# Expert weights as two fp16 parts made on chip, row stores issued by GpSimd, and score products on all 128 rows, in a two-layer attention and mixture-of-experts kernel

## The chip, the cores and the metric

One core of a Trainium2 chip runs the whole kernel. The metric is the device time of one execution in microseconds (us). Work runs on TensorE (PE in the profile; its weight loads are PEld), VectorE (DVE), ScalarE (ACT), GpSimd (POOL) and SyncE (SP), which here does little but issue DMAs. Sixteen DMA engines move data between memory and the chip.

## The reference, cut to what matters

Two layers. Each mixes the tokens (1024 latent ones of width 1024, and 256 context ones) by three groups of heads, of which two are attention with a softmax over scores, and then sends every token to two of 32 experts. One expert is a SwiGLU unit with three fp32 matrices of 2 MB each:

```python
s_loc = jnp.einsum('bnqhgd,bnkhd->bnhgqk', qb, kb) * ATTN_SCALE      # head width 64
...
p = softmax(concat([s_loc, s_ctx, sink_col], -1), -1)
...
def expert_block(args):
    xk, e = args            # rows of one expert; w_gate, w_up: 1024 x 512, w_down: 512 x 1024
    return (jax.nn.silu(xk @ w_gate[e]) * (xk @ w_up[e])) @ w_down[e]
```

Layer 0 sends 1280 tokens to experts, layer 1 only the 1024 latent ones.

## The kernel before

**Stages.** Each layer runs through the input projection, the recurrent heads, attention, the output projection, the routing, the experts and the combination of the experts' rows. On the span of the profiled execution, attention lies at about 732 to 1036 us in layer 0 and 2551 to 2827 us in layer 1, and the experts that are loaded by a run-time index start at 1232 and 2998 us.

**Attention.** Queries and keys are kept as a high and a low fp16 part of 64 rows each (one row for each entry of a head). The tile qs holds the high part in rows 0 to 63 and the low part in rows 64 to 127; k1 holds the keys' high part twice, in both halves; kl holds the keys' low part once, in rows 0 to 63. A score tile is the sum of a product on 128 rows (L1149: both parts of qs against k1) and one on 64 rows (L1150: the high part of qs against kl), for pieces of 256 or 128 keys. After it come the bias and maximum on DVE (L1162), the exponential on ACT (L1168), the normalization on GpSimd (L1179), transposes on PE (L1182, L1187), their copies on ACT and DVE (L1183), and the products with the values (L1192). The keys come by the DMAs k<-Bk and kl.

**Experts.** `PROFILE` and `FIXBLK` fix how many units of 32 rows each rank of expert gets. Of the 29 experts that are loaded by index, layer 0 gives 29 at least one unit, 19 at least two, 12 at least three, 12 four, 7 five, 5 six, 4 seven and 1 eight; in layer 1 the counts are 29, 18, 13, 6, 3, 2, 1, 1, 1, 1. Three more experts are fixed: their weights are loaded ahead of the stage, and they have 2, 2 and 3 units in layer 0, and 1, 2 and 1 in layer 1. In all that is 96 units in layer 0 and 79 in layer 1. An expert's units are worked in blocks of 128 rows and a rest of 64, 64 and 32, or 32 rows.

For an expert, `expert_load` issues three DMAs on SP (L1580: wg, wu, wd, 2 MB each) into one of three sets of buffers (two slots of pool wpa, and wp with wp2), taken in turn. For a block, `expert_rows` gathers the rows (L1592, an indirect DMA on GpSimd), transposes them and copies them to hT. `expert_block` multiplies them by wg and wu in fp32 (L1618). Each fp32 product appears as two instructions of the same columns. Blocks of 64 rows put wg and wu side by side in two column groups, and blocks of 32 rows use four. Its second half, `down`, applies silu (L1623), multiplies (L1624), transposes (L1628), copies gT (L1631, L1633), multiplies by wd (L1639), copies the result to y (L1643 and near) and stores it on SP (L1651 for 128 rows, L1653 for fewer). `down` of one block is issued after the first half of the next. In layer 1 the tile y has two buffers, in layer 0 three.

**What sets the order.** Instructions run in the order of each engine's queue. A DMA queue on SP also runs in order, so an SP DMA that waits for its tile holds back those behind it. `order_end` estimates the end of a sequence of experts from constants for a load and for the columns, and `expert_order` picks a sequence by it.

**After the experts**, the rows of ys are gathered on GpSimd (L1737) and combined.

## Time and profile before

| | |
|---|---|
| Median of 3 runs | 3684.35 us (3678.03 to 3684.88) |
| Profiled execution: its own time | 3684.05 us |
| Profiled execution: its span | 3682.0 us |
| PE busy | 3146.3 us (85% of the span) |
| DVE, ACT, POOL busy | 1787.3, 1090.0, 915.9 us (49%, 30%, 25%) |
| Granted TensorE clock, mean | 0.91 |
| DMA, mean over the span | 208 GB/s |

The profile gives busy time by engine, and the span in windows with the busy time, the granted TensorE clock and the busy share of the DMA engines. The averages run over stages with different limits, so the windows of a stage are read rather than the whole. In the views, L followed by a number is a line of the kernel, and "<-" behind a time of idleness names what ended it.

### The profile page before, as it was taken

Reading aid. Unit: us, or ns where it says so; the run is one execution under the profiler, and the core shown is the slowest. Engines: PE = TensorE matmul, PEld = TensorE weight load, DVE = VectorE, ACT = ScalarE, POOL = GpSimd, SP = SyncE. Lnnn points to the kernel's source line nnn. Section 1 sums busy time; section 2 is a strip of 40 time slices with the busy share of each in tenths; the row PEclk is TensorE's granted clock in tenths of the full one; section 3 lists DMA queues with packets and bytes.
Section 4 is the critical chain, followed back from the end, with each engine's and each line's share of the span. In section 5 each row is a group of like instructions: output and inputs, shape, how many; then the busy total and the mean of one; then the engine's idle time right before and its main releaser. Section 6 shows DMA issues by size and latency. Waiting matters only on the chain. (4 is left out here: it accounts for less than half of the span.)

```text
span 3682.0 us, 67190 instructions
## 1 busy us (share of the span) xinstructions
PE 3146.3 (85%) x26916; PEld 1837.6 (50%) x26916; DVE 1787.3 (49%) x4387; ACT 1090.0 (30%) x2416; POOL 915.9 (25%) x912
## 2 busy tenths in 40 slices
PE   7998889999997889999738988898999879986773
PEld 4656557656654344444326655675655444432331
DVE  4357777377668311111186677773755841110115
ACT  4333334346533100000045433442554310000001
POOL 2023433143324100000073244331432410000003
PEclk9989889989998899999968987997999879997987
DMA  9864333552264889989762533335331778899885
GB/s 361 298 185 113 88 87 95 147 152 67 79 206 166 275 334 360 368 347 358 293 223 74 158 94 98 94 89 163 96 106 57 254 238 344 330 386 360 308 317 196
DMA packets 456087, 770.06 MB, mean 209 GB/s; under 512 B 194398, under 2 KB 328830, under 8 KB 439134
## 3 DMA queue, kind: packets, MB, share of 16 engines
q1 hardware_dynamic: 442206, 718.16, 56.2%
q0 software_dynamic: 12848, 44.97, 3.8%
q8 instruction: 214, 3.51, 0.4%
q10 hardware_dynamic: 720, 2.62, 0.2%
q14 instruction: 99, 0.81, 0.1%
HBM read 650.68 MB, written 114.97 MB: 208 GB/s over the span
## 5 line engine op out<-in xcount | busy, mean ns | idle before, releaser
L1618 PE MATMUL pgate<-wg,hT 128*32 128x256 f32 (+2 forms) x1968 | 532.4, 487 | 85.9 <-issue 31.8
L1618 PEld LDWEIGHTS pgate<-wg,hT 128*32 128x32 f32 (+2 forms) x1968 | 196.3, 135 | 349.9 <-issue 287.7
L1618 PE MATMUL pgate<-wu,hT 128*32 128x256 f32 (+1 forms) x1648 | 361.6, 462 | 10.2 <-DMA wu<-w_up 10.2
L1639 PE MATMUL pd<-wd,gT 128*32 128x256 f32 (+2 forms) x1968 | 321.8, 472 | 51.7 <-DVE gT L1631 25.8
L514 PE MATMUL acc<-hL,wH 128*128 128x256 f16 (+2 forms) x1040 | 345.5, 333 | 16.3 <-POOL hL L471 16.2
L513 PE MATMUL acc<-hH,wH 128*128 128x256 f16 (+2 forms) x1040 | 343.3, 334 | 7.2 <-DVE hH L470 6.4
L515 PE MATMUL acc<-hH,wL 128*128 128x256 f16 (+2 forms) x1040 | 344.9, 333 | 0.0
L1623 ACT ACTIVATE sg<-pgate 64x256 f32<-64x256 f32 (+2 forms) x86 | 43.1, 501 | 980.3 <-PE pgate L1618 980.3
L1592 POOL DMA_INDIRECT xg<-hmoe,map x69 | 62.3, 903 | 1037.5 <-PE ptg L1628 566.3
L1179 POOL TENSOR_SCALAR s<-s,rd 128x640 f32<-128x640 f32 (+2 forms) x216 | 171.6, 795 | 288.4 <-DVE rd L1175 115.8
L1639 PEld LDWEIGHTS pd<-wd,gT 128*32 128x32 f32 (+2 forms) x1968 | 127.1, 130 | 208.7 <-issue 123.0
L1624 DVE TENSOR_TENSOR sg<-sg,pgate 64x256 f32<-64x256 f32 (+1 forms) x66 | 35.6, 540 | 344.4 <-ACT sg L1623 340.9
L1168 ACT ACTIVATE s<-s,nm 128x640 f32<-128x640 f32 (+2 forms) x216 | 164.4, 764 | 45.8 <-DVE nm L1165 39.8
L1277 PE MATMUL acco<-wo,o 128*128 128x512 f16 x756 | 176.5, 387 | 0.0
L1192 PE MATMUL po<-pt,vt 128*64 128x128 f32 x1920 | 168.6, 291 | 7.3 <-DVE pt L1183 6.5
L1618 PE MATMUL pup<-wu,hT 128*128 128x512 f32 x320 | 165.4, 605 | 9.6 <-DMA wu<-w_up 9.6
L1149 PE MATMUL pss<-k,qs 128*128 128x256 f16 (+1 forms) x552 | 153.2, 278 | 17.3 <-DMA k<-Bk 13.4
L1624 DVE TENSOR_TENSOR sg<-sg,pup 128x512 f32<-128x512 f32 x20 | 13.8, 688 | 292.1 <-PE pup L1618 292.1
L1618 PEld LDWEIGHTS pgate<-wu,hT 128*32 128x32 f32 (+1 forms) x1648 | 134.3, 123 | 42.1 <-issue 21.1
L1150 PE MATMUL pss<-kl,qs 64*128 64x256 f16 (+1 forms) x552 | 152.6, 277 | 0.0
L515 PEld LDWEIGHTS <-wL 128*128 128x128 f16 (+1 forms) x1040 | 104.9, 101 | 87.4 <-issue 26.7
L513 PEld LDWEIGHTS <-wH 128*128 128x128 f16 (+1 forms) x1040 | 105.4, 101 | 75.4 <-issue 19.7
(406 smaller groups left out, 6435.3 us busy)
## 6 DMA issues: line engine op xcount, KB each, us to landing
wu<-w_up SPq DMA_DIRECT2D x64, 2048.0 KB
wd<-w_down SPq DMA_DIRECT2D x64, 2048.0 KB
wg<-w_gate SPq DMA_DIRECT2D x64, 2048.0 KB
wmod<-w_mod SPq DMA_DIRECT2D x96, 512.0 KB
w<-w_in SPq DMA_DIRECT2D x41, 512.0 KB
ld<-ys SPq DMA_DIRECT2D x40, 384.0 KB
z<-inv SPq DMA_DIRECT2D x80, 128.0 KB
ys<-y SPq DMA_DIRECT2D x20, 512.0 KB
```

The costliest lines, as they stand in the source:

```text
L513: self.nc.tensor.matmul(ov, H[:, k, :], hh, start=k == 0, stop=False)
L514: self.nc.tensor.matmul(ov, H[:, k, :], hl, start=False, stop=False)
L515: self.nc.tensor.matmul(ov, Lo[:, k, :], hh, start=False, stop=k == KD - 1)
L1149: te.matmul(pss[:, o:o + n], qs[:, e, Q], k1[:, e, k0:k0 + n], start=True, stop=False)
L1150: te.matmul(pss[:, o:o + n], qs[0:64, e, Q], kl[:, e, k0:k0 + n], start=False, stop=True)
L1168: a.activation(s2[:, e, :nk], s2[:, e, :nk], AF.Exp, bias=nm[:, e:e + 1], scale=1.0 / SS, accum_out=den[:, e:e + 1])
L1179: g.tensor_scalar(s2[:, e, :nk], s2[:, e, :nk], rd[:, e:e + 1], SC_Q, OP.mult, OP.mult)
L1192: te.matmul(po[64 * e:64 * e + 64, 0:P], vt[:, kb, 64 * e:64 * e + 64], pt[:, e, x * P:x * P + P], start=x == 0, stop=x == len(kbs) - 1)
L1277: te.matmul(acc, o[:, zo, k] if k < KD - 1 else self.og_last[:, zo, tok], wo[:, zw, k, c], start=k == 0 and y == 0, stop=k == KD - 1 and y ...
L1592: nc.gpsimd.indirect_dma_start(out=xg[:m], out_offset=None, in_=self.h2[l], in_offset=bass.IndirectOffsetOnAxis(ap=idx, axis=0))
L1618: te.matmul(o[off + i * m:off + i * m + m, :n], hT[:, k], w[:, k, i * n:i * n + n], start=k == 0, stop=k == KD - 1)
L1639: te.matmul(o, gT[:, k, :m], wd[:, k, i * n:i * n + n], start=k == 0, stop=k == 3)
```

## The change

The change has four parts.

- **Experts.** A loaded expert with two or more units (19 in layer 0, 18 in layer 1) loads its fp32 weights into the buffers wp and wp2, which serve as a stage. `expert_split` then writes them as two fp16 parts into a slot of wpa: ACT makes the high parts (L1611, two instructions of 128 x 2048 for each matrix) and DVE the low parts (L1612, likewise). The rows hT and the silu product gT are made as two fp16 parts as well, and each fp32 product becomes three fp16 products (high by high, high by low, low by high). Experts with one unit load straight into a slot of wpa and stay in fp32, as do the fixed ones.
- **Order.** The first half of a block is cut into `gates(0)` and `gates(1)`; the silu, transposes and copy of the block before (`middle`) stand between the two. `order_end` has new constants and the rule of two slots and a stage, so the sequence of experts differs.
- **Stores.** The rows y are stored by GpSimd's queue (L1713, L1715) rather than SP's. In layer 0 ACT makes all of y, in layer 1 DVE.
- **Attention.** kl is loaded into both halves, by two DMAs, and the second score product runs on all 128 rows of qs, so it also adds low by low.

```diff
@@ order_end
-W_LOAD, W_ROWS, W_COL = 17.5, 0.75, (0.0, 6.9, 11.9, 18.8, 22.2)
+W_LOAD, W_PART = 16.5, 13.5
+W_COL = ((0.0, 6.9, 11.9, 18.8, 22.2), (0.0, 5.6, 9.6, 15.2, 17.5))
...
@@ attention
-                kl = qp.tile([64, 2, T], F16, tag="kl", name="kl", bufs=1 if B else 2)
-                nc.sync.dma_start(kl, kd[1])
+                kl = qp.tile([P, 2, T], F16, tag="kl", name="kl", bufs=1 if B else 2)
+                for z in range(2):
+                    nc.sync.dma_start(kl[64 * z:64 * z + 64], kd[1])
...
-                        te.matmul(pss[:, o:o + n], qs[0:64, e, Q], kl[:, e, k0:k0 + n], start=False, stop=True)
+                        te.matmul(pss[:, o:o + n], qs[:, e, Q], kl[:, e, k0:k0 + n], start=False, stop=True)
...
@@ experts
+    def expert_split(self, ws, wp):
...
+        for w, tag in zip(ws, ("wg", "wu", "wd")):
+            k, n = w.shape[1:]
+            t = wp.tile([P, 2, k, n], F16, tag=tag, name=tag + "p")
+            for k0 in range(0, k, k // 2):
+                c = slice(k0, k0 + k // 2)
+                nc.scalar.mul(t[:, 0, c], w[:, c], SC_W)
+                nc.vector.scalar_tensor_tensor(t[:, 1, c], w[:, c], SC_W, t[:, 0, c], OP.mult, OP.subtract)
+            out.append(t)
+        return out
...
+        parts = ((0, 0), (0, 1), (1, 0)) if split else ((None, None),)
...
+        def gates(half):
+            for k in range(4 * half, 4 * half + 4):
+                for y, (zh, zw) in enumerate(parts):
...
-                    loaded[r] = self.expert_load(l, e, wps[i % len(wps)])
+                    loaded[r] = self.expert_load(l, e, wps[2 if split(r) else 0])
+                    if split(r):
+                        loaded[r] = self.expert_split(loaded[r], wps[0][0])
...
-                nc.sync.dma_start(dst, y)
+                nc.gpsimd.dma_start(dst, y)
...
-                down = self.expert_block(l, loaded[r], hT[:, :, o:o + m], m, xp, ps, tag, ps_t, tag_t, self.ys[l][row:row + m])
+                gates, middle, down = self.expert_block(l, loaded[r], hT, o, m, xp, ps, tag, ps_t, tag_t, self.ys[l][row:row + m], split(r))
+                gates(0)
+                if pending:
+                    pending[0]()
+                gates(1)
...
+                    pending[1]()
+                pending = middle, down
```

On SP's queue in the experts of layer 0 the loads and the stores are mixed before (ys_83 is the rows' buffer of layer 0; the ISA rows are register work ahead of a DMA):

```order
L1580 DMA wu<-w_up 128x4096
L1651 DMA ys_83<-y 128x1024
L1580 ISA
L1580 DMA wd<-w_down 128x4x1024
L1580 ISA
L1580 DMA wg<-w_gate 128x4096
L1653 DMA ys_83<-y 4x32x256
```

The queue of SP now holds in this place only the loads; the stores have gone from it.

On GpSimd's queue, at the same place of the changed kernel, the stores stand between the gathers of the rows of later blocks:

```order
L1715 DMA ys_83<-y 4x32x256
L1620 DMA xg<-hmoe_79,map_13966 128x1024
L1715 DMA ys_83<-y 4x32x256
L1713 DMA ys_83<-y 128x1024
L1620 DMA xg<-hmoe_79,map_13966 96x1024
L1715 DMA ys_83<-y 2x64x512
```

Before, only the gathers (L1592) stood in this queue.

On ACT's queue in the experts of layer 0, before:

```order
L1623 ACTIVATE sg<-pgate 128x512
L1601 COPY hT<-ptx 128x4x96
L1623 ACTIVATE sg<-pgate 64x512
L1650 COPY y<-pd_14544 128x512
L1623 ACTIVATE sg<-pgate 64x256
```

And in the changed kernel (wgp, wup and wdp are the tiles of an expert's fp16 parts, made from the staged wg, wu and wd):

```order
L1611 ACTIVATE wup<-wu 128x2048 x2
L1670 ACTIVATE sg<-pgate 64x512
L1632 ACTIVATE hT<-ptx 128x8x64
L1711 ACTIVATE y<-pd_14987 128x256
L1688 CAST gT<-ptg 128x4x64
L1611 ACTIVATE wdp<-wd 128x2048 x2
L1670 ACTIVATE sg<-pgate 64x512
L1611 ACTIVATE wgp<-wg 128x2048 x2
L1632 ACTIVATE hT<-ptx 128x512 x2
```

The high parts of an expert to come now stand among the silu, the rows and the results of the experts that run.

## Rows read from the trace of the kernel before

**Rows 1.** windows: length; busy PE, PEld, DVE, ACT, POOL; PEclk, DMA share, GB/s
```profile
732.00:1036.00 304.00, 294.20 (x2276) 179.75 (x2273) 205.88 (x650) 166.73 (x453) 118.76 (x147) 0.95 0.33 93
1232.00:1823.00 591.00, 553.28 (x3256) 249.70 (x3256) 78.91 (x146) 47.79 (x93) 31.41 (x35) 0.99 0.91 350
2551.00:2827.00 276.00, 270.11 (x2058) 165.75 (x2060) 172.74 (x520) 144.15 (x370) 97.43 (x118) 0.91 0.38 111
2998.00:3586.00 588.00, 473.25 (x3266) 211.63 (x3256) 71.33 (x140) 35.63 (x74) 26.90 (x30) 0.92 0.88 341
```

**Rows 2.** timeline of PE in attention: start us, us, line, operands, shapes
```profile
863.39 0.28 PE L1149 MATMUL pss<-k,qs 128*128 128x256 f16 x1
863.60 0.28 PE L1150 MATMUL pss<-kl,qs 64*128 64x256 f16 x1
863.81 0.23 PE L1149 MATMUL pss<-k,qs 128*128 128x128 f16 x1
863.98 0.23 PE L1150 MATMUL pss<-kl,qs 64*128 64x128 f16 x1
```

**Rows 3.** timeline of PE, input projection: the same columns
```profile
51.86 0.27 PE L513 MATMUL acc<-hH,wH 128*128 128x256 f16 x1
51.97 0.27 PE L514 MATMUL acc<-hL,wH 128*128 128x256 f16 x1
```

**Rows 4.** L1149: count, ns min/median/max; in 2551:2827: busy us, mean ns, idle before
```profile
L1149 PE MATMUL pss<-k,qs x552: 219/282/421, 732.1 to 2815.7; 128*128 128x256 f16 x160, 128*128 128x128 f16 x24
...
L1149 PE MATMUL pss<-k,qs 128*128 128x256 f16 x192 | 56.8, 297 | 13.4 <-DMA k<-Bk 13.4
```

**Rows 5.** timeline of PE, expert products in fp32
```profile
1228.05 0.59 PE L1618 MATMUL pgate<-wg,hT 128*64 128x512 f32 x1
1228.05 0.59 PE L1618 MATMUL pgate<-wu,hT 128*64 128x512 f32 x1
1228.47 0.59 PE L1618 MATMUL pgate<-wg,hT 128*64 128x512 f32 x1
```

**Rows 6.** DMA issues: weights, stores of 64-row and 32-row blocks
```profile
wg<-w_gate SPq DMA_DIRECT2D x64, 2048.0 KB
...
ys<-y SPq DMA_DIRECT2D x29, 256.0 KB
...
ys<-y SPq DMA_DIRECT2D x37, 128.0 KB
```

**Rows 7.** windows late in the two expert stages, columns as rows 1
```profile
1790.00:1800.00 10.00, 9.02 (x52) 3.42 (x50) 1.56 (x3) 1.18 (x2) 0.00 (x0) 1.00 1.01 397
1815.00:1820.00 5.00, 4.64 (x66) 2.09 (x62) 0.69 (x1) 0.31 (x1) 0.00 (x0) 1.00 0.13 51
3600.00:3610.00 10.00, 0.00 (x0) 0.00 (x0) 1.34 (x2) 0.00 (x0) 0.00 (x0) 0.50 0.13 51
```

**Rows 8.** timeline: first weights issued, last products, first gather, each layer
```profile
1231.83 0.36 SPq L1580 DMA_DIRECT2D wg<-w_gate  x1
...
1821.30 1.93 PE L1639 MATMUL pd<-wd,gT 128*32 128x256 f32 x32 [0.39 <-DVE gT L1633]
...
1840.96 0.95 POOL L1737 DMA_INDIRECT cy<-ys,slot  x1 [6.18 <-DMA ys<-y]
...
2998.31 0.38 SPq L1580 DMA_DIRECT2D wg<-w_gate  x1
...
3593.48 1.93 PE L1639 MATMUL pd<-wd,gT 128*32 128x256 f32 x32 [2.69 <-DVE gT L1633]
...
3618.08 0.94 POOL L1737 DMA_INDIRECT cy<-ys,slot  x1 [93.52 <-ACT dg L1771]
```

**Rows 9.** waits of the second expert stage: us in total, times, longest
```profile
DVE y L1643 <- DMA ys<-y: 163.5, 26, 19.1
```

**Rows 10.** lines L1212 and L1213: count, ns min/median/max, shapes
```profile
L1212 ACT ACTIVATE wo<-wos x16: 1041/1060/1067, 903.7 to 2728.9; 128x1024 f16<-128x1024 f32 x16
...
L1213 DVE SCALAR_TENSOR_TENSOR wo<-wos,wo x16: 1196/1213/1564, 905.9 to 2731.1; 128x1024 f16<-128x1024 f32 x16
```

More of the change, by code (lines that the diff above doesn't have):

```diff
@@ L63, in units_of_rank @@
     return [sum(r < t for t in PROFILE[l]) for r in range(NE - NFIX)] + list(FIXBLK[l])
-W_LOAD, W_ROWS, W_COL = 17.5, 0.75, (0.0, 6.9, 11.9, 18.8, 22.2)
+SPLIT = 2
+W_LOAD, W_PART = 16.5, 13.5
+W_COL = ((0.0, 6.9, 11.9, 18.8, 22.2), (0.0, 5.6, 9.6, 15.2, 17.5))
 def order_end(units):
-    pe, dma, done = 10.0, 0.0, []
+    pe, dma, part = 10.0, 0.0, 0.0
+    slots, stage = [0.0, 0.0], 0.0
     for i, n in enumerate(units):
-        if i >= NFIX:
-            dma = max(dma, done[i - 3] if i >= 3 else 0.0) + W_LOAD
-            pe = max(pe, dma + 1.5)
-        dma += W_ROWS * n
-        pe += W_COL[4] * (n // 4) + W_COL[n % 4]
-        done.append(pe)
+        split = i >= NFIX and n >= SPLIT
+        if i < NFIX:
+            ready = 0.0
+        elif split:
+            dma = max(dma, stage) + W_LOAD
+            part = max(dma + 4.5, slots[0] + W_PART, part + W_PART)
+            ready, stage = part, part - 9.0
+        else:
+            dma = max(dma, slots[0]) + W_LOAD
+            ready = dma + 1.5
+        pe = max(pe, ready) + W_COL[split][4] * (n // 4) + W_COL[split][n % 4]
+        if i == NFIX - 1:
+            stage = pe
+        else:
+            slots = slots[1:] + [pe]
     return pe
@@ L1614, in expert_block, with part, middle @@
         h = max(q // 2, 1)
-        for k in range(KD):
-            for w, o, off in ((wg, pg, 0), (wu, pu, h * m if q > 1 else 0)):
-                for i in range(h):
-                    te.matmul(o[off + i * m:off + i * m + m, :n], hT[:, k], w[:, k, i * n:i * n + n], start=k == 0, stop=k == KD - 1)
-        def down():
-            r = h * m
-            sg = xp.tile([P, 512], F32, tag="sg", name="sg", bufs=2)
-            a.activation(sg[:r, :n], pg[:r, :n], AF.Silu)
-            v.tensor_tensor(sg[:r, :n], sg[:r, :n], (pu[r:2 * r] if q > 1 else pu)[:, :n], OP.mult)
+        r = h * m
+        parts = ((0, 0), (0, 1), (1, 0)) if split else ((None, None),)
+        def part(x, z):
+            return x if z is None else x[:, z]
+        def gates(half):
+            for k in range(4 * half, 4 * half + 4):
+                for y, (zh, zw) in enumerate(parts):
+                    for w, p, off in ((wg, pg, 0), (wu, pu, r if q > 1 else 0)):
+                        for i in range(h):
+                            te.matmul(p[off + i * m:off + i * m + m, :n], part(hT, zh)[:, k, o:o + m], part(w, zw)[:, k, i * n:i * n + n],
+                                      start=k == 0 and y == 0, stop=k == KD - 1 and y == len(parts) - 1)
+        got = {}
+        def middle():
+            sg = xp.tile([P, 512], F32, tag="sg", name="sg", bufs=2)
+            s = 1.0 / (SC_H * SC_W) if split else 1.0
+            a.activation(sg[:r, :n], pg[:r, :n], AF.Silu, scale=s)
+            pr = (pu[r:2 * r] if q > 1 else pu)[:, :n]
+            if split:
+                v.scalar_tensor_tensor(sg[:r, :n], pr, s, sg[:r, :n], OP.mult, OP.mult)
+            else:
+                v.tensor_tensor(sg[:r, :n], sg[:r, :n], pr, OP.mult)
             pt = ps_t.tile([P, 512], F32, tag=tag_t, name="ptg")
@@ L1636, in down @@
             for k in range(4):
[L1637 to L1639 removed]
+                for y, (zh, zw) in enumerate(parts):
+                    for i in range(max(q, 2)):
+                        t = (p0, p1)[i] if q == 1 else p0[i * m:i * m + m, :n]
+                        te.matmul(t, part(gT, zh)[:, k, :m], part(wd, zw)[:, k, i * n:i * n + n],
+                                  start=k == 0 and y == 0, stop=k == 3 and y == len(parts) - 1)
             y = self.yp.tile([P, D], F32, tag="y", name="y", bufs=2 if l == DEPTH - 1 else 3)
             ge = self.ge.get(q)
[L1642 to L1655 removed]
+            s = 1.0 / SC_W if split else 1.0
+            for p, c in ((p0, slice(0, n)), (p1, slice(512, 1024)))[:2 if q == 1 else 1]:
+                if ge is not None:
+                    v.scalar_tensor_tensor(y[:, c], p[:, 0:n], s, ge[:, c], OP.mult, OP.mult)
+                else:
+                    a.mul(y[:, c], p[:, 0:n], s)
+            if q == 1:
+                nc.gpsimd.dma_start(dst, y)
+            else:
+                nc.gpsimd.dma_start(dst.rearrange("t (i c) -> i t c", i=q), y[:, 0:n])
+        return gates, middle, down
     def experts(self, l, wps, xp, ps, tag, ps_t, tag_t, rest):
@@ L1712, in experts @@
                 if pending:
-                    pending()
-                pending = down
+                    pending[1]()
+                pending = middle, down
             if j == 2:
                 rest(xp, ps_t, tag_t)
-        pending()
+        for f in pending:
+            f()
         overflow()
```

58 lines of the change are left out of this document (33 added, 25 removed).

## The prediction, made before the changed kernel ran

> **What bounds the kernel now.** I read the windows of the four stages that the change touches first, then the instructions of their bound engine in order of time, then the transfers, and last how each expert stage begins and ends. The two attention stages are bound by PE: it is busy 294.20 of 304 us in layer 0 and 270.11 of 276 in layer 1, against 205.88 and 172.74 for DVE, the next engine, and a DMA share of a third [rows 1]. The two expert stages are bound by transfers. Their DMA share is 0.91 and 0.88 at 350 and 341 GB/s, while the best stretch near their end runs 397 GB/s [rows 1, 7]. PE is close behind in layer 0 (553.28 of 591 us) and not in layer 1 (473.25 of 588). DVE and ACT are nearly idle there (78.91 and 47.79 us of 591), which is the room into which the change puts its work.
>
> The missing bandwidth has a shape. Where the loads are over and only stores of short blocks run, the share is 0.13, about 2 of 16 engines, at 51 GB/s [rows 7]. There are 29 stores of 256 KB and 37 of 128 KB [rows 6], so what is behind them on those engines waits for them while the others are idle.
>
> **Attention.** The change replaces the 64-row product by a 128-row one of the same columns. Before, products of 256 columns that alternate between 128 and 64 rows start 0.21 us apart, and of 128 columns 0.17 us [rows 2]. Two 128-row fp16 products of 256 columns in the input projection start 0.11 us apart [rows 3], so 128 columns would take about 0.055 (estimate). Each of the two changes the weights as well. So both sizes lose about 0.106 us for each product if the alternation is what holds them, and there are 552 of either kind [rows 4]: 1104 x 0.106 = 117 us, or 61 and 56 us when shared by the stages' PE time. This is the upper bound. Next, what is late after it: with 233 us of PE work in layer 0, DVE's 205.88 us need 254 us at a density of 0.81, which I estimate as what this chain can keep (it holds 0.68 and 0.63 now); that gives -50. In layer 1 PE's 214 us at a density of 0.93, a little under its 0.97 now, give 230 and -46. Against this stands the second DMA of kl: PE waits 13.4 us once in layer 1 for the keys [rows 4], and one more DMA lies in the same queue. I take 6 us for it, so **-90 us**. If DVE cannot hold more than 0.70, layer 0 needs 294 us and layer 1 247, and only 10 + 29 = 39 us are gained; that is the lower bound.
>
> The order in which products follow each other is also where the Trainium skill speaks against the change: "TensorE: Matmul & The Clock Gate", Part 3 on row and column tiling, states that weight loads overlap with products in flight only when the row group differs. By it the products on all rows would not close up, and the term would be 0. The trace disagrees: the 0.11 us start to start of rows 3 is between two products on all 128 rows with different weights.
>
> **Experts, PE.** An fp32 product of 512 columns is two recorded instructions (a down product of 32 rows, 4 by 4 pieces, counts x32 [rows 8]), each 0.42 us after the one before [rows 5]: 0.86 us. Three fp16 products of 512 columns, at twice 0.11, are 0.65. A block of 128 rows has 24 products, so it falls from 20.6 to 15.6 us; a block of 64 from 10.3 to 7.8, one of 32 by 1.2. By the table of units, layer 0 splits 13, 11 and 5 such blocks (some 100 us less), layer 1 7, 14 and 8 (some 80 us less). PE then has about 455 of the 591 and 395 of the 588 us. It stands below the transfers in both layers, so I give this term nothing by itself: it is cover for the rest.
>
> **Experts, the split.** The nearest rows are the same two operations in the output projection: 1.060 us on ACT and 1.213 us on DVE for 128x1024 [rows 10]. An expert has 12 times this size: 12.7 us on ACT and 14.6 us on DVE. A load of 6.29 MB at 397 GB/s takes 15.8 us, so both splits fit under it. Over 19 and 18 experts DVE goes from 78.91 to about 356 us of work in layer 0 and from 71.33 to about 334 in layer 1. They cost nothing while they lie beside a load; the rival below says what they cost if not.
>
> **Experts, the transfers.** 29 loads of 6.29 MB and 96 units with 0.262 MB each (gather and store of 32 rows of 4 KB) are 207.6 MB in layer 0, and 203.2 MB with 79 units in layer 1. At 397 GB/s these are 523 and 512 us. Two engines carry the stores of 64-row blocks, 14 in layer 0 and 15 in layer 1, at 0.131 MB on each of the two; with these the fuller engines have about 14.6 and 14.4 MB at a sixteenth of the 397 GB/s, so 588 and 581 us. The stages have 583 us until only stores run (1232 to 1815) and 588 (2998 to 3586) [rows 1, 7]. So the two engines explain the whole loss by size. A second cause lies beside it: in layer 1 DVE waits 163.5 us for stores before it may write y [rows 9]. The change moves the stores to GpSimd's queue. What the trace of before doesn't show is which engines that queue uses for a row of 64 parts. Bounds: the same two, and no gain; or all in turn, and the whole 60 to 76 us. I take the second, since the loads then have SP's queue to themselves in any case.
>
> On the second, the Trainium skill ("DMA: Bandwidth & Descriptors", on why a DMA increments its semaphore by 16) states that a hardware queue takes the lowest-numbered engines and a software queue takes them from a cursor that goes round. The trace agrees with the first half (0.13 [rows 7]); no run here shows the other.
>
> To the 523 and 512 us come waits for the stage and the two slots: a split must have ended before the stage is refilled. Between 0 and 40 us a layer; I take 14 and 8, one short load's worth. From the last landing to PE's end I take 14 us, a split of one matrix (5 us) and a block of 64 rows. Layer 0: 1231.83 + 523 + 14 + 14 = 1783, against 1823.2 now (the last products start at 1821.30 and last 1.93) [rows 8]: -40. Layer 1: 2998.31 + 512 + 8 + 14 = 3532, against 3595.4: -63. Then the first gather of the combination, which waits for the stores, comes 17.7 us after PE's end in layer 0 and 22.7 in layer 1 (1840.96 and 3618.08 [rows 8]). These are short stores one behind the other, 5 us for 256 KB at 51 GB/s. With spread stores I take 11 us, so -7 and -12. **Layer 0 -47, layer 1 -75.** At 40 us of waits they are -21 and -43.
>
> **Stores on GpSimd** cost that engine an issue for each block, beside gathers of 0.9 us. A store that waits for its y holds back the gathers queued behind it, and through them the transposes of a later block. In the order of the changed kernel the gathers stand some three blocks ahead of their use, so 30 us and more of PE's work cover it, and I cost it at nothing; without the cover it would be the wait for one block's second half, some 5 us each.
>
> **The sum**, against the profiled execution's own 3684.05 us (its span is 3682.0; the median of the runs is 3684.35, so it is a typical one): -90 - 47 - 75 = -212, **3472 us**. A measurement of this kernel can tell about 0.2%, 7 us, from no change.
>
> **The rivals.**
>
> *DVE's chain bounds attention.* Against the main case only the attention term changes, to -39: 3523 us. For it: DVE, ACT and GpSimd follow each other in every block, and DVE is at 0.68 already. Against it: PE waits for next to nothing now. Chance 0.13.
>
> *Products on all rows don't close up* (the page's rule above). Attention gives 0: 3684 - 122 = 3562 us. The trace speaks against it [rows 3]. Chance 0.04.
>
> *The stores move their queue and not their engines*, so that this part of the change doesn't do what it says. The loads keep their 583 and 588 us; attention and the shorter ends remain: 3684 - 90 - 19 = 3575 us. Chance 0.10.
>
> *More than that.* Attention at its upper bound of 117, no waits for slots, tails of 5 us: -117 - 67 - 89 gives 3411 us. Chance 0.11.
>
> *Slower: splits stand ahead of the running expert.* ACT and DVE run their queues in order. If a split of wd, say, stands ahead of the silu of the running block and its weights haven't landed, silu, gT and PE wait: 2.1 MB of landing at 397 GB/s (5.3 us) and 4.9 us for four DVE pieces, 10.2 us. For 37 experts that is 377 us, and with the other terms 3684 + 377 - 212 = 3849 us. It decides from 212/37 = 5.7 us an expert on. For it: the two queues in the order shown have the splits among the silu and the copies. Against it: the split stands after a silu whose products come later than the landing at the pace of the loads. Chance 0.05. A half of this price that just eats the gain, 3684 us, has 0.02.
>
> **How the numbers follow.** The main case has 0.55 and its own range is 3435 to 3505 us, by 30 us of waits for slots and 7 to 27 us of attention either way. The range of 8 in 10 takes in the main case, DVE's chain, the rule and the unmoved engines (0.82): 3420 to 3580 us. It leaves out the larger gain and the two bad ones. Faster 0.93, same 0.02, slower 0.05.
>
> **What would show it.** Attention: starts of the score products 0.11 us apart, the stages at 254 and 230 us and DVE's density near 0.8; with unchanged starts the term is wrong, with close starts and idle PE it is DVE's chain. Experts: windows at about 390 GB/s, PE at 455 and 395 us, DVE at 356 and 334, no wait of DVE for ys; a share of 0.13 where only stores run would say that the engines are unmoved, and PE waiting for silu behind a split would say the slower rival. The forecast is wrong if the expert stages end later than 1810 and 3575 us less what attention gave ahead of them.

## The result, and the profile after

The changed kernel takes 3565.44 us (median of 4 runs, 3555.23 to 3581.03), against 3682.19 us of the kernel before (4 runs, 3678.03 to 3684.88): a ratio of 0.9688, 95% interval 0.9667 to 0.9710. That is 117 us less. The prediction had 3472 us and the range 3420 to 3580: the time lies in the range, near its slow end, but 60 us outside the main case's own 3435 to 3505, and the gain is little more than half of the 212 us that the sum gave. The profiled execution took 3569.75 us (span 3568.1).

The page of the changed kernel: the busy time by engine, then the span in 40 slices with the busy tenths of PE, DVE and ACT, the granted clock, and the DMA engines' share.

```profile
PE 2943.9 (83%) x28620; PEld 1838.5 (52%) x28620; DVE 2283.7 (64%) x4614; ACT 1544.1 (43%) x2769; POOL 996.8 (28%) x998
...
PE   7998888989997888888737988898889867777875
DVE  4257777467768474547688677783776845555765
ACT  4334344346633153546544434343465314434641
PEclk9989899989998889899868988899899978889977
DMA  9864343372455889999862432443732769999976
```

PE fell by 202 us of work and DVE rose by 496. In the expert stages PE is at 0.8 in most slices of the first (the 14th to the 20th) and at 0.7 in most of the second (the 33rd to the 39th).

The windows of the four stages, with the columns of [rows 1], the expert stages from the first load issued to the last product:

```profile
734.00:1004.00 270.00, 244.20 (x2270) 182.45 (x2268) 201.85 (x651) 165.05 (x453) 119.28 (x146) 0.94 0.40 112
1199.50:1779.20 579.70, 489.00 (x4068) 238.39 (x4064) 323.23 (x243) 292.99 (x293) 72.88 (x76) 0.92 0.94 358
2501.50:2742.00 240.50, 213.63 (x2065) 164.14 (x2066) 172.79 (x520) 142.19 (x371) 99.13 (x118) 0.94 0.47 133
2910.60:3499.90 589.30, 451.26 (x4284) 228.46 (x4280) 327.20 (x278) 249.94 (x227) 64.02 (x73) 0.85 0.91 344
```

Set beside [rows 1], the attention stages became shorter by 34 and 36 us (303.7 to 269.9 and 276.6 to 240.4 from the first to the last product). The expert stages took 591.4 and 597.1 us from first load to last product before, and take 579.7 and 589.4 now. Their DMA share is 0.94 and 0.91, against 0.91 and 0.88 in [rows 1].

The last products and the first gather of the combination, in layer 0 and in layer 1, which answer to [rows 8]:

```profile
1775.75 3.50 PE L1702 MATMUL pd<-wd,gT 128*32 128x256 f32 x32 [1.15 <-DMA wd<-w_down]
...
1787.95 1.03 POOL L1814 DMA_INDIRECT cy<-ys,slot  x1 [5.68 <-DMA ys<-y]
...
3496.43 3.51 PE L1702 MATMUL pd<-wd,gT 128*32 128x256 f32 x32 [2.72 <-DMA wd<-w_down]
...
3508.65 1.02 POOL L1814 DMA_INDIRECT cy<-ys,slot  x1 [6.46 <-DMA ys<-y]
```

The gather comes 8.7 us after PE's end in both layers (17.7 and 22.7 before).

Put together by matched points (first score product, last attention product, first expert product, last expert product, first gather, end of the span), the difference of the two spans is this:

| stretch | forecast, us | measured, us |
|---|---|---|
| start to the first score product | 0 | +1.9 |
| attention, layer 0 and layer 1 | -90 in all | -33.8 and -36.2 |
| attention to experts, both layers | 0 | -0.6 |
| experts, first to last product | -40 and -63 | -11.7 and -9.6 |
| last product to first gather | -7 and -12 | -9.0 and -14.0 |
| gather to attention of layer 1, gather to the end | 0 | +3.5 and -4.4 |
| all | -212 | -114 |

So 82 of the missing 98 us are missing in the two expert stages.

### The profile page after: what moved, and what is told of

The parts are those of the page before. It is cut to its first block, busy times and chain, and to the rows that moved or that the text cites. A ratio compares the mean times of both kernels' runs of the same rounds, so it can differ in the third digit from the quotient of the medians.

```text
span 3568.1 us, 71262 instructions
## 1 busy us (share of the span) xinstructions
PE 2943.9 (83%) x28620; PEld 1838.5 (52%) x28620; DVE 2283.7 (64%) x4614; ACT 1544.1 (43%) x2769; POOL 996.8 (28%) x998
## 5 line engine op out<-in xcount | busy, mean ns | idle before, releaser
L1662 PE MATMUL pgate<-wgp,hT 128*64 128x512 f16 (+2 forms) x1704 | 371.7, 388 | 130.8 <-ACT wgp L1611 76.6
L1662 PEld LDWEIGHTS <-hT 128*64 128x64 f16 (+2 forms) x3408 | 210.9, 110 | 365.9 <-issue 195.5
L1662 PE MATMUL pgate<-wup,hT 128*32 128x256 f16 (+1 forms) x1224 | 212.8, 362 | 24.5 <-DVE wup L1612 13.7
L1702 PE MATMUL pd<-wdp,gT 128*64 128x512 f16 (+2 forms) x1704 | 213.1, 358 | 21.7 <-DVE gT L1689 14.9
L1612 DVE SCALAR_TENSOR_TENSOR wgp<-wg,wgp 128x2048 f16<-128x2048 f32 x74 | 166.6, 2286 | 93.4 <-ACT wgp L1611 93.4
L1612 DVE SCALAR_TENSOR_TENSOR wdp<-wd,wdp 128x2048 f16<-128x2048 f32 x74 | 166.6, 2288 | 71.8 <-ACT wdp L1611 71.8
L1612 DVE SCALAR_TENSOR_TENSOR wup<-wu,wup 128x2048 f16<-128x2048 f32 x74 | 166.2, 2287 | 31.1 <-ACT wup L1611 31.0
L1611 ACT ACTIVATE wgp<-wg 128x2048 f16<-128x2048 f32 x74 | 137.6, 1903 | 74.1 <-DMA wg<-w_gate 56.7
L1611 ACT ACTIVATE wdp<-wd 128x2048 f16<-128x2048 f32 x74 | 137.2, 1902 | 73.7 <-DMA wd<-w_down 69.3
L1715 POOL DMA_DIRECT2D ys<-y x66 | 51.8, 784 | 384.4 <-DVE y L1709 215.5
L1611 ACT ACTIVATE wup<-wu 128x2048 f16<-128x2048 f32 x74 | 137.3, 1904 | 44.4 <-DMA wu<-w_up 41.7
```

What stands on the lines that cost most here:

```text
L1611: nc.scalar.mul(t[:, 0, c], w[:, c], SC_W)
L1612: nc.vector.scalar_tensor_tensor(t[:, 1, c], w[:, c], SC_W, t[:, 0, c], OP.mult, OP.subtract)
L1662: te.matmul(p[off + i * m:off + i * m + m, :n], part(hT, zh)[:, k, o:o + m], part(w, zw)[:, k, i * n:i * n + n], start=k == 0 and y == 0, ...
L1702: te.matmul(t, part(gT, zh)[:, k, :m], part(wd, zw)[:, k, i * n:i * n + n], start=k == 0 and y == 0, stop=k == 3 and y == len(parts) - 1)
```

## The experiments

The lengths of the stages in the table are those of one profiled execution, from the first expert product to the last. Where a stretch is said to go from the first load, it starts later than that: by some 10 us in layer 0 and 16 to 18 in layer 1 in most kernels, and by 1 us in layer 0 of e5 and e6, whose first products are fewer. Experts of layer 1 in e9 are left out, since the rows of layer 0 are other numbers there and change the routing; in e5 and e6 the same holds, and layer 1 is given for its transfers alone.

| kernel | time, us | ratio to before, 95% | experts L0, L1, us |
|---|---|---|---|
| before | 3682.19 | 1 | 601.2, 614.7 |
| changed | 3565.44 | 0.9688 (0.9667 to 0.9710) | 589.5, 605.1 |
| e1: before + attention | 3599.71 | 0.9783 (0.9754 to 0.9811) | 600.2, 625.2 |
| e2: before + GpSimd stores | 3614.12 | 0.9824 (0.9793 to 0.9855) | 581.1, 581.7 |
| e3: changed, SP stores | 3615.60 | 0.9834 (0.9790 to 0.9879) | 621.3, 631.7 |
| e4: changed, no split | 3516.81 | 0.9554 (0.9521 to 0.9587) | 565.6, 577.9 |
| e5: before, few products | 3677.09 (one run) | | 599.9, 597.0 |
| e6: e5 + GpSimd stores | 3528.59 (one run) | | 542.4, 538.7 |
| e7: changed, high parts alone | 3457.66 (one run) | | 547.3, 555.6 |
| e8: changed, one product of three | 3485.11 (one run) | | 557.8, 573.1 |
| e9: changed, no low parts, three products | 3512.06 (one run) | | 559.2 |
| e10: split of 5 units and more | 3623.56 | 0.9842 (0.9820 to 0.9864) | 637.5, 617.2 |
| e11: e4 with two sets | 3583.34 (one run) | | 601.1, 597.2 |
| e12: e4, other planner constants | 3503.45 | 0.9506 (0.9473 to 0.9540) | 566.9, 566.4 |

My first reading of the two traces was theory B: the DMA engines are at 0.94 already, so the transfers have a floor near 555 us that the prediction had missed with its 397 GB/s, and the stores' engines matter little. The first four runs were made to test that against the prediction's own step.

**e1, attention alone.**

```diff
-                kl = qp.tile([64, 2, T], F16, tag="kl", name="kl", bufs=1 if B else 2)
-                nc.sync.dma_start(kl, kd[1])
+                kl = qp.tile([P, 2, T], F16, tag="kl", name="kl", bufs=1 if B else 2)
+                for z in range(2):
+                    nc.sync.dma_start(kl[64 * z:64 * z + 64], kd[1])
...
-                        te.matmul(pss[:, o:o + n], qs[0:64, e, Q], kl[:, e, k0:k0 + n], start=False, stop=True)
+                        te.matmul(pss[:, o:o + n], qs[:, e, Q], kl[:, e, k0:k0 + n], start=False, stop=True)
```

> The kernel before with the attention part of the change alone (kl in both halves, the second score product on all 128 rows). Theory A (what the two traces show: products close up to 0.11 us, and the stages get 34 and 36 us shorter because PE then waits for DVE's chain now and then): about 70 us less than before, 3612 us. Rival (the prediction's term, the shortfall in the changed kernel being due to the other parts): 90 us less, 3592 us.

Measured: 80 us less, just between the two (70 to 91 by the interval), so the run decides for neither. The attention stages are 265.3 and 237.9 us from first to last product, 77 us less in all. The experts of layer 1 came out 10 us longer to their last product, but the first gather follows it after 12.0 us in place of 22.7: from the first expert product to that gather it is 637.3 us, and 637.4 before, so nothing was lost there.

**e2, the stores alone.**

```diff
-                nc.sync.dma_start(dst, y)
+                nc.gpsimd.dma_start(dst, y)
...
-                nc.sync.dma_start(dst.rearrange("t (i c) -> i t c", i=q), y[:, 0:n])
+                nc.gpsimd.dma_start(dst.rearrange("t (i c) -> i t c", i=q), y[:, 0:n])
```

> The kernel before with the stores of rows moved to GpSimd's queue alone. Theory B (the engines' work per byte, about 555 us of all sixteen in each expert stage, and not two overfull engines, bounds the transfers; the short ends after PE's last product are the gain): 20 to 35 us less than before, about 3655 us, expert stages from first load to last product 580 to 595 us. Rival (the prediction's step: two engines overfull with 64-row stores hold the loads): stages 540 to 560 us and 90 to 110 us less in all, about 3580 us.

Measured: 66 us less, twice and more what theory B gave. The stages got 20 and 33 us shorter. From first load to last product, as the numbers above are meant, they are 571.3 and 564.1 us: below theory B's 580 to 595 and above the rival's 540 to 560. In fp32, though, PE alone has some 550 us of products in layer 0, so in that layer this run cannot tell what the transfers could do.

**e3, the changed kernel with the stores back on SP.** The edit is that of e2 backwards.

> The changed kernel with the stores of rows back on SP's queue. Theory B: the expert stages stay within 15 us each and the ends come back (9 and 18 us): 3590 to 3600 us. Rival (two overfull engines): the stages get 20 us and more longer each: 3620 us or more.

Measured: 3615.60 us, 50 us more than the changed kernel, and the stages 32 and 27 us longer. That is the rival's number for the stages, while the time lies between the two (3600 and 3620). Theory B is in doubt from the other side too.

**e4, no split.** Everything else is as in the changed kernel, but for the planner, whose rule and constants are those of before, and the three sets, which are taken in turn as before.

```diff
-SPLIT = 2
+SPLIT = 99
...
-W_LOAD, W_PART = 16.5, 13.5
-W_COL = ((0.0, 6.9, 11.9, 18.8, 22.2), (0.0, 5.6, 9.6, 15.2, 17.5))
+W_LOAD, W_ROWS, W_COL = 17.5, 0.75, (0.0, 6.9, 11.9, 18.8, 22.2)
...
-                    loaded[r] = self.expert_load(l, e, wps[2 if split(r) else 0])
+                    loaded[r] = self.expert_load(l, e, wps[i % len(wps)])
```

> The changed kernel without the split: all experts in fp32, three sets of buffers in turn and the planner's constants as before; attention, stores and the place of the silu are as in the changed kernel. Theory B (transfers bound the expert stages, so the split buys little): within 15 us of the changed kernel, 3555 to 3580 us. Rival C (PE's 553 of 591 us held layer 0, and the split is what gave its gain): 20 us or more slower than the changed kernel, 3585 us or more. Rival D (the split's stage and two slots hold back loads): 15 us or more faster, 3550 us or less.

Measured: 3516.81 us, 49 us faster than the changed kernel, and the intervals of the two ratios lie apart. This is rival D's number: the split, which was the largest part of the change, costs time, together with the order of experts that goes with it. The windows of e4's expert stages, columns as before, from first load to last product:

```profile
1197.90:1753.70 555.80, 552.67 (x3252) 250.13 (x3248) 55.38 (x103) 69.78 (x134) 63.02 (x76) 1.00 0.97 373
2875.70:3436.80 561.10, 486.86 (x3389) 213.51 (x3387) 75.94 (x148) 36.65 (x76) 60.49 (x73) 0.94 0.95 360
```

In layer 0 PE is busy 552.67 of 555.80 us in fp32: without the split PE is the bound there, at a full clock, and still the stage is 24 us shorter than with it.

**e5 and e6, the transfers alone.** To see what the transfers do when nothing holds them, most products were left out of the kernel before: of each sum over 8 or 4 pieces only the first was multiplied. e6 has GpSimd's queue for the stores besides, as in e2.

```diff
-        for k in range(KD):
+        for k in range(1):
...
-            for k in range(4):
+            for k in range(1):
```

> The kernel before with most expert products left out: only the first of the 8 and of the 4 pieces of the inner dimension is multiplied, in every block, so that PE is out of the way and the loads, gathers and stores run at their own pace. Read is layer 0, from the first load to the last product (591 us before). Theory B: 550 to 570 us. Rival (two engines overfull with the 64-row stores): 580 to 590 us. Rival C (PE holds the stage, the transfers could do 397 GB/s): about 530 us.

> The same with the stores of rows on GpSimd's queue. Theory B: within 10 us of the run with stores on SP. Rival (two overfull engines): 50 us and more shorter than that run.

Measured, layer 0 from first load to last product, e5 and then e6:

```profile
1223.00:1821.80 598.80, 251.07 (x932) 103.38 (x932) 84.53 (x167) 48.47 (x95) 33.39 (x35) 0.58 0.90 346
```

```profile
1221.10:1762.40 541.30, 261.54 (x932) 107.34 (x932) 83.83 (x167) 47.84 (x95) 65.35 (x77) 0.59 1.00 384
```

With PE at less than half of its work e5 still takes 598.8 us, no less than the kernel before (591.4; from the first product on, 599.9 and 601.2): there the stores on SP's queue were the bound. Moving them alone takes 57.5 us off, and the DMA share goes from 0.90 to 1.00 and the rate from 346 to 384 GB/s. Theory B falls. The two overfull engines of the prediction hold up in size in layer 0 (588 us forecast for the fuller engines, 598.8 measured to the last product), and so does its floor (523 us of transfers and 14 at the end, measured 541.3 in all).

The midst of e5's stage also has stretches in which only two or three of the sixteen engines work (a share of 0.16 is 2.6 engines), such as this one, with nothing on PE:

```profile
1476.00:1481.00 5.00, 0.00 (x0) 0.00 (x0) 0.00 (x0) 0.00 (x0) 0.00 (x0) 0.50 0.16 64
```

By the times of the packets in the traces, exactly two are in flight for 7% of e5's stage and for 1% of e6's, and there is next to no time with none. The same edit also takes the stores out of the loads' queue, where a store that waits for its y holds back the loads behind it (SP waits 102 us for the tiles of stores in e5). The runs don't part this from the overfull engines.

**e7, e8 and e9, the split taken apart.** All three are the changed kernel. e7 has no low parts of weights (DVE's half of the split) and one product in place of three; e8 keeps the whole split and has one product; e9 has no low parts, but three products, each with the high part.

```diff
-                nc.vector.scalar_tensor_tensor(t[:, 1, c], w[:, c], SC_W, t[:, 0, c], OP.mult, OP.subtract)
...
-        parts = ((0, 0), (0, 1), (1, 0)) if split else ((None, None),)
+        parts = ((0, 0),) if split else ((None, None),)
```

> The changed kernel with only the high parts of the split weights: DVE makes no low part of a weight, and one product stands in place of three for the split experts (the two products with low parts are left out). The rest of the chain, load to stage, ACT's split, slot, is kept. Read are the expert stages from the first load to the last product (580 us in layer 0). Theory B: 555 to 575 us, since the transfers alone take that. Rival D (the split's chain and the slots that PE frees hold the loads back): 540 us or less.

> The changed kernel with the split whole (ACT's high and DVE's low parts are made), but one product in place of three for the split experts (the products with low parts are left out). Read are the two expert stages from the first expert product to the last (589.5 and 605.1 us in the changed kernel, 547.3 and 555.6 with the high parts alone). Theory D1 (the split on DVE is the long step between a slot that comes free and the next product): 575 us or more in layer 0. Rival D2 (the time of PE's products, which holds the slots, and not the split on DVE): 555 us or less.

> The changed kernel with no low parts of the weights, but three products all the same (each with the high part): PE's time is kept, DVE's part of the split is gone. Theory D1: 555 us or less in layer 0. Rival D2: 575 us or more. If both matter in turn, between 555 and 575 in this run and in the run with one product.

Measured, layer 0 from first load to last product, e7, e8, e9:

```profile
1190.00:1727.60 537.60, 326.59 (x2440) 148.76 (x2440) 70.77 (x130) 292.51 (x294) 63.79 (x77) 0.75 0.99 385
```

```profile
1190.00:1738.20 548.20, 331.38 (x2436) 150.93 (x2432) 322.93 (x243) 292.28 (x293) 71.24 (x76) 0.75 0.99 378
```

```profile
1193.50:1742.90 549.40, 478.62 (x4068) 240.77 (x4064) 70.91 (x129) 292.82 (x293) 62.84 (x76) 0.93 0.98 378
```

With neither, layer 0 takes 537.6 us at a DMA share of 0.99, which is rival D's number: the stage and the slots, with ACT's half of the split and the changed kernel's order of experts, are no hindrance there by themselves. Taking away DVE's half alone gives 549.4 us, PE's two products alone 548.2, and the changed kernel with both has 579.7. So neither D1 nor D2 is right alone. In layer 0 either of them is nearly hidden; together they are not (10.6 us and 11.8 us from e7, but 42.1 for both). By the numbers given ahead for layer 0 (555 and less, 575 and more, from the first product) both runs fall between, 557.8 and 559.2, as the text for e9 allowed. In layer 1 DVE's half costs more by itself: 573.1 us in e8 against 555.6 in e7. Each of the three is a single run.

**e11, two sets of buffers.** e4 with two sets for the loaded experts in place of three:

```diff
-                    loaded[r] = self.expert_load(l, e, wps[i % len(wps)])
+                    loaded[r] = self.expert_load(l, e, wps[0])
```

> The kernel without a split (3517 us) with two sets of buffers for the loaded experts in place of three. Read are the two expert stages from the first expert product to the last (565.6 and 577.9 us with three sets, 589.5 and 605.1 in the changed kernel, whose products see two slots). Theory E (the split costs its time because products are left with two sets and the loads run less far ahead): both stages at or above the changed kernel's, 590 us or more and 605 us or more. Rival (the third set matters little; the splits' work is the cost): within 10 us of 565.6 and 577.9.

Measured: 601.1 and 597.2 us, against 565.6 and 577.9 with three sets: 55 us for the two stages, and 66 us more in all, by one run. The sequence of experts is still the one that the planner made for three sets. Layer 0 is above the changed kernel, as theory E has it, and layer 1 is 8 us below it. The third set is worth 20 to 35 us a layer in this kernel. In layer 0, from the first load:

```profile
1203.20:1793.00 589.80, 564.06 (x3228) 250.41 (x3228) 55.18 (x103) 69.78 (x134) 63.03 (x76) 0.98 0.92 351
```

**e10, a split for the largest experts only.** Experts of five units and more are split (10 in all), the others stay in fp32 and take whichever of the three sets was used longest ago; the planner's constants are those of before.

```diff
-SPLIT = 2
+SPLIT = 5
...
-                    loaded[r] = self.expert_load(l, e, wps[2 if split(r) else 0])
+                    if split(r):
+                        k, sets[:] = 2, [sets[1], i, -9]
+                    elif sets[0] < sets[2]:
+                        k, sets[:] = 0, [sets[1], i, sets[2]]
+                    else:
+                        k, sets[2] = 2, i
+                    loaded[r] = self.expert_load(l, e, wps[k])
```

> The changed kernel with a split only for experts of five or more units (7 in layer 0, 3 in layer 1); the others go in fp32 through all three sets of buffers, the set that was used longest ago first, with the planner's constants as before. Theory D (what the split costs goes with the number of split experts, 37 here down to 10, while PE's relief in layer 0 stays for the largest): about the time without a split, 3517 us, or up to 15 us below it, 3500 to 3520 us. Rival (each split of a large expert holds its slot and the stage as before): 3535 us or more.

Measured: 3623.56 us, 107 us more than with no split at all, the rival's number. The theory that the cost goes with the number of split experts falls. A split expert takes two of the three sets, the stage while it loads and a slot as long as it runs, and here an fp32 expert may sit in the stage, so that a load to be split waits for that expert's last product. In layer 0 from the first expert product PE has 539.88 us of work in 638 us and the DMA engines a share of 0.86:

```profile
1175.00:1813.00 638.00, 539.88 (x3824) 250.19 (x3824) 164.94 (x190) 161.59 (x209) 64.49 (x78) 0.92 0.86 326
```

That the sets are the cause here is argued from the code; the planner, which knows nothing of the split in this kernel, may have its part, and the run does not separate the two.

**e12, e4 with the planner's constants as measured.**

```diff
-W_LOAD, W_ROWS, W_COL = 17.5, 0.75, (0.0, 6.9, 11.9, 18.8, 22.2)
+W_LOAD, W_ROWS, W_COL = 16.0, 0.67, (0.0, 6.9, 11.9, 18.8, 22.2)
```

> The kernel without a split (3517 us) with the planner's two transfer constants as the runs with GpSimd stores measured them (16.0 us a load and 0.67 us a unit in place of 17.5 and 0.75), which moves the expert of ten units in layer 1 from the head of the sequence towards its middle. If the order in layer 1 (PE without a pause for its first 180 us, then transfers without a pause) costs what lies between 577.9 us and the 539 us of the run with products left out: 15 to 25 us less, 3495 to 3502 us. If not: within 8 us of 3517 us.

Measured: 3503.45 us, 13 us less than e4 by the medians, with intervals of the two ratios that overlap (0.9473 to 0.9540, and 0.9521 to 0.9587). It lies between the two numbers given ahead, so the run doesn't settle what the order costs. The stage of layer 1 went from 577.9 to 566.4 us. What was looked for in e4's layer 1 were windows like these two, of 60 us each, early and late:

```profile
2978.00:3038.00 60.00, 60.00 (x308) 27.32 (x301) 8.92 (x16) 4.07 (x8) 6.50 (x8) 1.00 0.91 360
3218.00:3278.00 60.00, 44.85 (x422) 18.91 (x418) 7.59 (x17) 2.79 (x6) 7.06 (x9) 0.91 1.02 380
```

Early, PE is never free and the DMA engines are at 0.91; late, the DMA engines are full and PE waits a quarter of the time. The new sequence moves the largest expert away from the head. Of the kernels that leave no product out this is the fastest, and it has no split: by its ratio some 182 us below the kernel before.

## Why the prediction came out as it did

**The range held, in part by luck.** The main case's own range, 3435 to 3505 us, was missed by 60 us. The wide range reached up to 3580 for the sake of two rivals, products on all rows that don't close up (3562) and stores that don't change their engines (3575). Neither came about: the time lies where they would have put it for other reasons, the split above all. Of its own signs, layer 0's experts should have ended by 1776 us (1810 less 34) and ended at 1779.25; layer 1's ended at 3499.9, before 3505. The sum of the faster rival is also 6 us off: its terms give -70 and -92 in place of -67 and -89, so 3405 us.

**Attention: the mechanism held, the size was 10 to 20 us off.** The score products start 0.11 to 0.12 us apart, as [rows 3] had it, and not 0.21 (TensorE in attention of the changed kernel; start, length, line, operands, shapes):

```profile
834.02 0.28 PE L1163 MATMUL pss<-k,qs 128*128 128x256 f16 x1
834.14 0.27 PE L1164 MATMUL pss<-kl,qs 128*128 128x256 f16 x1
834.25 0.38 PE L1201 MATMUL pp<-c,s 128*128 128x128 f32 x2
834.47 0.27 PE L1163 MATMUL pss<-k,qs 128*128 128x256 f16 x1
834.58 0.27 PE L1164 MATMUL pss<-kl,qs 128*128 128x256 f16 x1
```

PE's work fell by 50.0 us in layer 0 (294.20 to 244.20; 61 forecast) and by about 57 in layer 1 (56 forecast). In layer 0 the term that was mis-sized is mainly this work: 244.20 us are left where the sum took 233. In layer 1 it is the density that was left, 0.89 where the sum took 0.93 (in layer 0 0.905 for 0.917), with DVE at 0.75 and 0.72 of the two stages, where the sum took 0.81 for layer 0. By itself this part takes 77 us off the two stages (e1; 80 us in all), in the changed kernel 70. The rival of DVE's chain (-39) did not come about. Nor did the Trainium skill's rule ("TensorE: Matmul & The Clock Gate", Part 3, weight loads overlap only between differing row groups): by it the starts would have stayed apart. But the prediction argued against it from the wrong pair: the two products of [rows 3] have the same weights, wH, and so have the two score products at 834.47 and 834.58 (qs). The rows that follow in the kernel before show it, since there the weights change from wH to wL and back:

```profile
51.97 0.27 PE L514 MATMUL acc<-hL,wH 128*128 128x256 f16 x1
52.08 0.27 PE L515 MATMUL acc<-hH,wL 128*128 128x256 f16 x1
52.19 0.27 PE L513 MATMUL acc<-hH,wH 128*128 128x256 f16 x1
```

These are products on all 128 rows with different weights, and they too start 0.11 us apart.

**The stores: right.** The step said that two engines carry the short blocks' stores and hold the loads, that the floor without this is 523 us, and that GpSimd's queue might not have it. e5 and e6 agree with each of the three: 598.8 us at 346 GB/s with the stores on SP, two packets at a time in its poor stretches, and 541.3 us at 384 GB/s without. The Trainium skill's sentence on software queues ("DMA: Bandwidth & Descriptors", on why a DMA increments its semaphore by 16: engines from a cursor that goes round) agrees with this, though no row here names the engines, and the 0.13 of [rows 7] says only that they are about two. In e2 the move gives 66 us by itself. In the changed kernel undoing it costs 50 (e3).

**PE's work in the experts as cover: right in direction, not in size.** PE has 489.00 us of work in layer 0, where 455 was forecast, and 451.26 in layer 1, where 395 was. The forecast took its products from rows at a full clock; the granted clock of the stages is 0.92 and 0.85. In the trace 64.1 of the 489.0 us and 127.0 of the 451 lie at a clock of 0.50 (1.2 GHz), and fp16 products of 512 columns on 128 rows start 0.426 us apart there, against 0.216 at 1.00 (2.4 GHz). With that part halved the work would be 457 and 388 us (estimates), close to the forecast. Before, the clock was 0.99 in layer 0 [rows 1], with a PE that hardly waited.

**The split: the step that failed.** The prediction costed it at nothing while it lies beside a load, and took 14 and 8 us for waits for the stage and the slots, with a bound of 40. With the transfers at 523 and 512 us and 14 at the end, the two stages show 43 and 63 us in that place (579.7 - 523 - 14, and 589.4 - 512 - 14). The floor itself was right: left alone, the transfers and their end take 541.3 and 525.8 us (e6), where the sum had 537 and 526. Not all of the 43 and 63 us go with the split, though: from first load to last product e4, without one, takes 555.8 and 561.1 us, 24 and 28 us less than the changed kernel. The durations were right: ACT and DVE need 1.90 and 2.29 us for 128 x 2048, 11.4 and 13.7 us an expert, below the 15.8 us of its load. The error is in what the comparison leaves out. A sum of work per engine that is below the load's says that the chain can keep pace on the average; it says nothing on how far ahead it runs. Before, the loads went into three sets in turn, and PE used them from there. Now the third set is a stage from which PE uses nothing in most experts, and the weights of an expert pass it in turn: the load, ACT's part, DVE's part, and only then the next load of that matrix. Before either part can be written, the slot must have come free from the expert two before.

The loads that wait on SP show the new step. In the expert stage of layer 0 of the changed kernel (what SP waited for, us in total, times, longest):

```profile
SPq L1594 <- PE pd L1702: 156.9, 10, 26.4
SPq L1594 <- PE pgate L1662: 75.4, 6, 25.9
SPq L1594 <- DVE wdp L1612: 69.0, 12, 15.2
SPq L1594 <- DVE wup L1612: 60.5, 11, 9.3
SPq L1594 <- DVE wgp L1612: 48.3, 8, 8.2
```

The last three lines, 178 us, have no counterpart before: a load that may not begin as DVE hasn't yet read the stage. They are not a loss one for one, since earlier loads are still landing meanwhile: e8, with one product for three, has 169 us of the same waits and a DMA share of 0.99. A stretch shows PE's side of it (ACT, DVE, PE and SP of the changed kernel; in brackets the idle time before, and what ended it):

```profile
1474.65 1.91 ACT L1611 ACTIVATE wgp<-wg 128x2048 f16<-128x2048 f32 x1 [2.20 <-DMA wg<-w_gate]
1476.59 2.29 DVE L1612 SCALAR_TENSOR_TENSOR wgp<-wg,wgp 128x2048 f16<-128x2048 f32 x1 [3.98 <-ACT wgp L1611]
1476.61 0.59 PE L1662 MATMUL pgate<-wgp,hT 128*64 128x512 f16 x1 [4.33 <-ACT wgp L1611]
...
1481.11 0.33 SPq L1594 DMA_DIRECT2D wg<-w_gate  x1
...
1482.87 0.59 PE L1662 MATMUL pgate<-wup,hT 128*64 128x512 f16 x1 [2.10 <-ACT wup L1611]
1485.19 0.59 PE L1662 MATMUL pgate<-wup,hT 128*64 128x512 f16 x1 [1.69 <-DVE wup L1612]
```

PE has no work until ACT has the first part of wg, then none until ACT and DVE have wu, and SP issues the next wg (1481.11) only when DVE has read the last one out (its two instructions on wg end at 1481.08). In some windows of 8 us around it and elsewhere in the stage, PE and the transfers take turns:

```profile
1376.00:1384.00 8.00, 8.00 (x88) 4.29 (x90) 1.27 (x3) 1.94 (x4) 1.64 (x2) 1.00 0.59 196
1392.00:1400.00 8.00, 1.28 (x6) 0.50 (x5) 0.71 (x2) 3.45 (x4) 0.57 (x1) 0.82 1.00 416
1472.00:1480.00 8.00, 3.67 (x35) 1.64 (x35) 3.70 (x3) 4.09 (x3) 0.78 (x1) 0.72 0.99 365
1480.00:1488.00 8.00, 4.21 (x24) 1.83 (x18) 5.60 (x4) 5.94 (x5) 0.74 (x1) 0.50 0.88 328
1512.00:1520.00 8.00, 8.00 (x139) 5.36 (x138) 3.00 (x5) 2.31 (x5) 2.65 (x3) 1.00 0.64 200
```

PE is full while the DMA engines are at 0.59 and 0.64, and has 1.28 of 8 us while they are at 1.00. These five are not the rule. Of the 71 such windows in layer 0, 10 have a DMA share under 0.8, and PE is full in 7 of these; the 12 in which PE is busy for less than 0.7 have a share of 0.98; in 25 both are at 0.95 and more. With a deeper queue of weights between them each should run through the other's pause; this is argued. e11 tests the depth without any split: with two sets the same kernel loses 66 us. And e7 to e9 show the other side in layer 0: a shorter chain (no DVE part) or shorter products (one for three) brings the transfers back to 0.98 and 0.99 of their time. What the runs don't settle is the share of the lost set and that of the added latency, since the split cannot be had here without its stage.

**The slower rival** put the cost of a split in front of the running expert at 10.2 us for each of 37. It did not come in that size. ACT's splits, which stand ahead of the silu, cost the transfers nothing by themselves: e7 keeps them and has its transfers at 0.99 in layer 0. The waits of PE in layer 0 of the changed kernel show both ways in which the split can delay it, the weights (wgp) and the chain behind the silu (sg); the largest of either kind (us in total, times, longest):

```profile
PE pgate L1662 <- ACT wgp L1611: 29.9, 7, 7.7
PE ptg L1679 <- DVE sg L1673: 16.7, 9, 6.3
```

All of the first kind make 48 us and all of the second 28, against 0 and 3 in e4. The second is 1.5 us for each of the 19 split experts, where the rival had 10.2. How much of either becomes time of the stage the runs don't separate. As rivals the prediction had a case for a loss of 377 us, and, in its sum, waits of 14 and 8 us with a bound of 40; the 43 and 63 us that came lie beyond that bound.

**The sum of the parts.** By the runs: attention -80 (e1), stores -66 (e2), split and its order of experts +49 (e4 against the changed kernel), and what remains of e4 over the first two, -19 (3682 - 80 - 66 - 3517). That rest is put down to the new place of the silu and to y on ACT in layer 0, which no run tests alone. Since it is a rest, the sum closes by itself and proves nothing. A gain of some 165 us came down to 117 by the part that was to bring the products' relief.

## What to carry to other kernels

A change that makes two buffers and a stage out of three buffers must be costed by how far the loads can run ahead, and not only by whether each engine's work fits under a load; draw the times of one set from the issue of its load to its release before giving a chain the price of nothing. Where a product is made cheaper, ask what its making delays: without the split PE held layer 0 (552.67 of 555.80 us), and with it PE had less work (489.00 us) and the stage was longer. A few short stores can set the pace of all the large loads on their queue: stores that alone keep a share of 0.13 busy held a whole stage at 0.90, and on another queue it ran at 1.00 (e5, e6).

## What the hardware showed unasked

- Left alone, the transfers of a 541 us stage run at a share of 1.00 and 384 GB/s from end to end (e6), although the gathers and the stores of another queue are mixed in.
- Where PE waits much, the granted clock is low: 0.58 and 0.59 of full speed in the mean of layer 0's stage of e5 and e6, and 0.50 in the window 1480 to 1488 of the changed kernel, the lower of its two levels. A PE that waits for weights is then also slow when they come: in layer 0 of the changed kernel, 64.1 of its 489.0 us of work lie at that level.
